# A two-layer streaming encoder on one core: the first MLP's down projection in seven products, one residual tile, and conditioning sums moved and widened

## The chip, the cores and the metric

The kernel runs on one core of one Trainium2 chip. The metric is the device time of one execution in microseconds (us), as the median of several executions of the same program. The core has five engines that run side by side, each with its own instruction stream in a fixed order: PE (matrix products, with PEld for its weight loads), DVE (elementwise work on 128 partitions), ACT (functions and copies), POOL, and SP, which here issues the transfers (DMA) between the chip's memory and the core's on-chip memory. An engine takes its instructions strictly in order: one that waits holds everything behind it. Instructions wait on semaphores that other engines raise.

## What is computed

The reference is one inference step with two layers over 1024 prompt rows and 32 sample rows of width 1024, all in float32. What matters here:

```python
def ada_mod(c, w, b):
    return jax.nn.silu(c) @ w + b
...
    for l in range(DEPTH):
        sh1, sc1, g1, sh2, sc2, g2 = jnp.split(ada_mod(c, p['w_ada'][l], p['b_ada'][l])[:, None, :], 6, axis=-1)
        u = x * (1 + sc1) + sh1
        ...
        x = layer_norm(ALPHA * x + (1 + g1) * y, p['ln_g'][l, 0], p['ln_b'][l, 0])
        u = x * (1 + sc2) + sh2
        f = jnp.square(jax.nn.relu(u @ p['w_up'][l])) @ p['w_down'][l]
        x = layer_norm(ALPHA * x + (1 + g2) * f, p['ln_g'][l, 1], p['ln_b'][l, 1])
```

Layer 0 mixes with a chunked matrix memory, layer 1 with banded attention that reads keys and values made from `ada_mod(c, w_ada_kv, b_ada_kv)`. Both layers end in the same MLP: up from 1024 to 4096 columns, squared relu, down to 1024. There are two conditioning vectors c, one for the prompt rows and one for the sample rows, so every `ada_mod` is a product of a 1024 x n matrix with two vectors; layer 1's matrix has 6144 columns and the keys' one 2048.

## The kernel before

All activations are kept transposed: 128 partitions hold a slice of the features, and the 1056 rows lie along the free axis. Float32 accuracy on PE is bought with three matmuls for each product: operands are split into a high and a low part, and high x high, high x low and low x high are accumulated (`proj`, line 111). PE works on 128 x 128 weights and a moving tile of up to 384 rows.

The order in time is: mixer of layer 0; its output projection (`out_proj` at line 1371); MLP of layer 0; queries, keys and values; attention; output projection of layer 1; MLP of layer 1; output norm.

MLP of layer 0 (`mlp`, line 1006) is plain. It takes the 4096 hidden columns in eight groups of 512. For each group it computes `up` on row blocks of 384, 384 and 288 (`TBS`), squares, splits into high and low, and multiplies by the group's part of w_down (`down`), which DVE adds into the residual: `add_gated_at`, line 986, one instruction for each result in PSUM. The hidden values stay on chip.

MLP of layer 1 (`mlp7`, line 1124) works on quarters of 264 rows (`QN`). Its up writes the hidden values of 14 of the 16 column blocks, already combined into the seven forms that a seven-product (Strassen-like) 2 x 2 scheme needs, to the chip's memory (`hd`), and the last two blocks plainly (`up_plain`, to `hpl`). Its down then runs in 16 units: four groups of column blocks (3, 4, 3 and 4 of them: `GRP`) times four pairs of output columns. `forms` (line 1217) loads a unit's weights (`rdn`) and makes their seven combinations with DVE and ACT; `fill` loads the hidden forms (`fx`) into room on chip that has come free, some of it the room of the up's input; `unit` (line 1263) issues seven products for each of two row pairs, and after each of them DVE adds its PSUM result into the residual. A product into a PSUM bank that DVE is still to read must wait for it. The two plain blocks follow at the end. PE's order within the 16 units is as written (`manual_schedule`), DVE, ACT and SP get theirs when the program is built.

The conditioning of layer 1 and of the keys is made during the MLP of layer 0, on DVE, because PE is busy (`ada_cols`, line 225, called by `ada_rest`, line 1373): 1 MB of weights comes for two column chunks of 128, in two loads; for each of eight blocks of 128 weight rows and both vectors one instruction of 256 columns multiplies and accumulates; then one transpose and one reduce. After every fourth pair four tiny matmuls on PE (`adas`, line 252) sum over partitions. The values go into `ada`, the norm's gains and shifts (`combine`) follow, and `bias_table` makes the attention's bias.

Such work is cut into pieces by a small planner, `Flow` (line 47). A task is a generator that yields a number; the main program calls `flow.tick(us)` after each of its own products. A tick subtracts its amount from the waits, and a task whose wait has come to zero or below goes one step and gets its next wait whole: what it was over is not carried on.

```python
            t[1] -= us
            if t[1] <= 0:
                wait = next(t[0], self)
                ...
                    t[1] = wait or 0.0
```

`flow.finish(task)` runs all that is left of a task at once, at that place of the program. The norms are such tasks too (`norm`, line 846), and `before0(ti)` and `end0` finish them where their result is needed.

The residual of layer 0 (`open_acc`, line 800) is three tiles, one for each row block, each in a pool of its own that closes when that block's norm is done. Their room is used again by the query tiles `QO`. Temporaries come from a pool of five tiles (`tmp_t`), raw weights from three (`raw_tile`), split weights from six.

## Time and profile before

| | us |
|---|---|
| median of 3 runs | 2479.84 |
| lowest and highest of them | 2478.87, 2482.77 |
| the profiled execution, its own time | 2483.94 |
| its span in the profile | 2482.1 |

The stages of the profiled execution, by the busy time of the engines in each:

| stage | from, to (us) | PE busy | DVE busy | ACT busy | DMA share |
|---|---|---|---|---|---|
| mixer of layer 0 | 0 to 421 | 401.07 | 354.29 | 221.88 | 0.41 |
| its output projection | 421 to 517.5 | 95.61 | 78.76 | 40.59 | 0.38 |
| queries | 1266 to 1362 | 95.31 | 77.35 | 62.95 | 0.30 |
| keys and values | 1362 to 1426 | 60.56 | 44.19 | 35.52 | 0.34 |
| attention | 1426 to 1640 | 201.49 | 147.65 | 136.09 | 0.12 |
| output projection of layer 1 | 1640 to 1733 | 88.99 | 53.48 | 43.24 | 0.32 |
| end of the last down, output norm | 2412 to 2482 | 56.56 | 52.15 | 15.09 | 0.29 |

The rows of the two MLPs, which stand between these, are shown where they are used. To read the views: a group of instructions is given by its line in the kernel, engine, operation, the tile it writes and the tiles it reads, the shape, how many there were (x), their busy time together, the mean length of one in ns, and the idle time of the engine ahead of them with what ended it. A matmul's length is from its start to its modelled end, and the next one starts before that: what a run of matmuls costs is its length in time divided by their count. A stage's row gives for each engine the busy time and the number of instructions, then the granted clock of PE, the share of the DMA engines' time and the bytes moved. In the chain of waits and in the timeline the first two numbers are start and length in us.

### The profile page before, as it was taken

The numbers are of one execution on the slowest core, as the hardware profiler recorded it, in microseconds if no ns is written. First come the engines' busy times: TensorE is split into PE (matmuls) and PEld (weight loads), VectorE is DVE, ScalarE is ACT, GpSimd is POOL, SyncE is SP. The second block draws the span as 40 slices with busy tenths as digits, with TensorE's granted clock in tenths as the row PEclk, the third lists the DMA queues.
The fourth block names the chain that finished last, engine by engine and source line by source line (L and its number), as shares of the span: only waits on it lengthen the run. The fifth ranks groups of instructions, "written<-read, shape, count | busy, mean of one in ns | idle before, by whom it ended". The sixth has DMA issues, their size and how long they took to land.

```text
span 2482.1 us, 42688 instructions
## 1 busy us (share of the span) xinstructions
PE 2416.0 (97%) x16844; PEld 2317.8 (93%) x16844; DVE 1764.3 (71%) x4046; ACT 1011.6 (41%) x2110; POOL 166.3 (7%) x315
## 2 busy tenths in 40 slices
PE   7999999999999999999999999999999999899997
PEld 4999999999999999999999967789999999899997
DVE  4899899788679679677597667746853443776758
ACT  4544456382212212212266566654754443221212
POOL 0211100000000000000000144410000000000003
PEclk9999999999999999999999999999999999999999
DMA  8433233313224224234122310051376557667632
GB/s 294 124 109 96 82 93 112 126 35 113 80 88 135 85 87 132 81 94 142 43 96 83 90 41 1 18 147 34 133 248 218 204 180 276 233 243 270 257 129 72
DMA packets 236220, 318.10 MB, mean 128 GB/s; under 512 B 11624, under 2 KB 185084, under 8 KB 234996
## 3 DMA queue, kind: packets, MB, share of 16 engines
q1 hardware_dynamic: 236020, 315.38, 38.8%
q8 instruction: 132, 2.16, 0.4%
q14 instruction: 68, 0.56, 0.1%
HBM read 242.79 MB, written 74.91 MB: 128 GB/s over the span
## 4 chain that ended last, share of the span: by engine, by line
PE 78%; DVE 8%; DMA 6%; ACT 2%; issue 1%; POOL 0%; SPq 0%; DVEq 0%; ACTq 0%; POOLq 0%
PE up L118 9%; PE up L120 9%; PE up L119 9%; PE dn L1278 9%; PE dn L119 5%; PE dn L118 5%; PE dn L120 5%; DMA fx<-hd 3%; PE pv L1599 2%; PE pt L1579 2%; PE s L1549 2%; PE o L118 1%; PE o L119 1%; PE o L120 1%; PE op_b L118 1%
## 5 line engine op out<-in xcount | busy, mean ns | idle before, releaser
L120 PE MATMUL up<-u,w_up 128*128 128x264 f32 x1024 | 292.9, 286 | 0.0
L118 PE MATMUL up<-u,w_up 128*128 128x264 f32 x1024 | 292.4, 286 | 0.0
L119 PE MATMUL up<-u,w_up 128*128 128x264 f32 x1024 | 291.1, 284 | 0.0
L1278 PE MATMUL dn<-fx,wf 128*128 128x264 f32 x2208 | 274.7, 286 | 10.7 <-DVE s L1242 8.0
L1278 PEld LDWEIGHTS dn<-fx,wf 128*128 128x128 f32 x2208 | 272.3, 190 | 11.9 <-DVE s L1242 8.1
L119 PE MATMUL dn<-h,w_dn 128*128 128x384 f32 (+1 forms) x768 | 249.5, 325 | 0.0
L118 PE MATMUL up<-U,w_up 128*128 128x384 f32 (+1 forms) x768 | 249.2, 324 | 0.0
L119 PE MATMUL up<-U,w_up 128*128 128x384 f32 (+1 forms) x768 | 247.9, 323 | 0.0
L118 PE MATMUL dn<-h,w_dn 128*128 128x384 f32 (+1 forms) x768 | 247.8, 323 | 0.0
L120 PE MATMUL up<-U,w_up 128*128 128x384 f32 (+1 forms) x768 | 247.6, 322 | 0.0
L120 PE MATMUL dn<-h,w_dn 128*128 128x384 f32 (+1 forms) x768 | 247.3, 322 | 0.0
L119 PEld LDWEIGHTS up<-u,w_up 128*128 128x128 f32 x1024 | 193.9, 189 | 0.0
L118 PEld LDWEIGHTS up<-u,w_up 128*128 128x128 f32 x1024 | 193.8, 189 | 0.0
L120 PEld LDWEIGHTS up<-u,w_up 128*128 128x128 f32 x1024 | 193.3, 189 | 0.0
L238 DVE SCALAR_TENSOR_TENSOR aacc<-rada,cs,aacc 128x256 f32<-128x256 f32 x448 | 190.2, 477 | 0.0
L986 DVE SCALAR_TENSOR_TENSOR ACC<-dn,ada,ACC 128x264 f32<-128x264 f32 (+4 forms) x328 | 131.8, 426 | 81.5 <-PE dn L1278 69.0
L986 DVE SCALAR_TENSOR_TENSOR acc<-dn,ada,acc 128x384 f32<-128x384 f32 (+2 forms) x256 | 119.4, 486 | 47.0 <-PE dn L120 45.9
L119 PEld LDWEIGHTS dn<-h,w_dn 128*128 128x128 f32 x768 | 144.5, 188 | 0.2 <-DVE h L1028 0.2
L1025 ACT ACTIVATE r<-up 128x384 f32<-128x384 f32 (+1 forms) x96 | 44.2, 462 | 246.3 <-PE up L120 237.7
L120 PEld LDWEIGHTS dn<-h,w_dn 128*128 128x128 f32 x768 | 144.5, 188 | 0.0
L120 PEld LDWEIGHTS up<-U,w_up 128*128 128x128 f32 x768 | 144.3, 188 | 0.0
L118 PEld LDWEIGHTS up<-U,w_up 128*128 128x128 f32 x768 | 144.2, 188 | 0.1
(354 smaller groups left out, 5959.7 us busy)
## 6 DMA issues: line engine op xcount, KB each, us to landing
hd<-HL SPq DMA_DIRECT2D x28, 1848.0 KB
raw_up<-in_w_up_dram SPq DMA_DIRECT2D x68, 512.0 KB
rada<-in_w_ada_dram SPq DMA_DIRECT2D x64, 512.0 KB
fx<-hd SPq DMA_DIRECT2D x37, 528.0 KB
raw_dn<-in_w_down_dram SPq DMA_DIRECT2D x36, 512.0 KB
ada_room<-in_w_ada_dram SPq DMA_DIRECT2D x32, 512.0 KB
fx<-hd SPq DMA_DIRECT2D x50, 264.0 KB
fx<-hd SPq DMA_DIRECT2D x16, 792.0 KB
```

The source lines that it names most:

```text
L118: nc.tensor.matmul(ps, wh, mov(0, k), start=(k == 0), stop=False)
L119: nc.tensor.matmul(ps, wh, mov(1, k), start=False, stop=False)
L120: nc.tensor.matmul(ps, wl, mov(0, k), start=False, stop=(k == nk - 1))
L238: nc.vector.scalar_tensor_tensor(acc[:, cnd], raw[:, k], sc, acc[:, cnd], op0=ALU.mult, op1=ALU.add)
L986: nc.vector.scalar_tensor_tensor(xs, ps[:, off + o:off + o + mm_], gate[:, fc, cnd:cnd + 1], xs, op0=ALU.mult, op1=ALU.add)
L1025: nc.scalar.activation(r, ps[:, :n], AF.Relu)
L1278: nc.tensor.matmul(p, ws[w][:, wl, k], t[:, s0, xl], start=first and k + n_ == 0, stop=k == kg - 1 and n_ == 2, skip_group_check=not first)
L1549: nc.tensor.matmul(s[:, b, :w], qst, kk[i][:, g, k0 + j0:k0 + j0 + w], start=(i == 0), stop=(i == 1))
L1579: nc.tensor.transpose(pt[:kp, j - j0, pr * P:(pr + 1) * P], ps_[pr][:, j * P:j * P + kp], ident)
L1599: nc.tensor.matmul(pv[64 * e:64 * e + 64, :nq], V[:kp, vt0 + j, g * 64:(g + 1) * 64], pts[e][:kp, j, :nq], start=(j == 0), stop=(j == nt - 1))
```

## The change

The first MLP uses `mlp7` as well, through a class `L0` that tells it where its input, rooms and row pairs are; `mlp` and `open_acc` go. The residual of layer 0 is one tile `ACC0` of 1056 rows, and its pool closes when all three norms are done, ahead of the second row block of the queries. Conditioning is made by a new function in three parts: 24 chunks of layer 1 and the keys' 16 during the first up (four chunks at once, 512 columns in an instruction, one load of 256 KB for each of the eight blocks of 128 weight rows), 16 chunks during the first down (two at once, 256 columns, a load of 256 KB for two of these blocks), and 8 during the second up (four at once). The order in `mlp7` between up and down and the time at which a unit's weights are asked for (`step`) change for both layers, and `forms` writes two of its sums over the raw weights.

```diff
+    def ada_more(src, c0, base, nch, nb, mk, tmp_f, step):
+        n = nb * P
+        kk_ = 512 // n
+        for j in range(0, nch, nb):
...
+            for k0 in range(0, KC, kk_):
+                raw = tmp_f([P, kk_, n], f"rada_{base}_{j}_{k0}")
+                nc.sync.dma_start(raw, src[k0 * P:(k0 + kk_) * P, c0 + j * P:c0 + (j + nb) * P].rearrange(
+                    "(k p) c -> p k c", p=P))
+                yield step[0]
+                for k in range(kk_):
+                    for cnd in range(2):
+                        sc = cs[:, k0 + k, cnd:cnd + 1]
+                        if k0 + k:
+                            nc.vector.scalar_tensor_tensor(accs_[cnd], raw[:, k], sc, accs_[cnd],
+                                                           op0=ALU.mult, op1=ALU.add)
...
+            yield step[1]
+            ada_sums(at, base, j, nb, mk)
...
-    ADA_B = (4.0, 2.0, 1.0)
+    ADA_U, ADA_D, ADA_1 = (3.2, 2.0), (7.5, 1.5), (6.0, 2.0)
-    W00 = (6.0, 12.0, 0.0, 0.0, 0.0, 3.0)
+    W00 = ((6.0, 12.0, 0.0, 0.0, 0.0, 3.0), (6.0, 12.0, 0.0, 0.0, 0.0, 3.0), (16.0, 14.0, 0.0, 0.0, 0.0, 3.0))
...
-            nc.vector.tensor_sub(s3, a11, a21)
-            nc.vector.tensor_sub(s4, a12, s2)
-            for x, y in ((s2, s1), (s3, s4)):
+            nc.vector.tensor_sub(a11, a11, a21)
+            nc.vector.tensor_sub(a12, a12, s2)
+            for x, y in ((s2, s1), (a11, a12)):
...
-        for pb in range(NW, NPB):
-            up_plain(pb, tp0)
+        for tp in L.pairs:
+            up_plain(NW, tp)
         prep(0)
+        up_plain(NW + 1, tp0)
+        for _ in range(4):
+            got[0] = next(preps[0])
+        prep(1)
         for t in L.rooms(tp0):
             rooms.add(t)
         fill(0, fx)
-        up_plain(NW, tp1)
-        for _ in range(4):
-            got[0] = next(preps[0])
         up_plain(NW + 1, tp1)
-        prep(1)
         for t in L.rooms(tp1):
             rooms.add(t)
         fill(0, fx)
+        L.down()
         with tc.manual_schedule(engines={mybir.EngineType.PE}):
...
-                    if j == 3:
+                    if j == 4:
                         prep(i + 2)
...
+    def ada_up():
+        yield from ada_more(a["w_ada"][1], 0, 48, 24, 4, mm, tmp_t, ADA_U)
+        yield from ada_more(a["w_ada_kv"], 0, 96, 16, 4, mm, tmp_t, ADA_U)
...
+        bias_table()
+    def ada_down():
+        yield from ada_more(a["w_ada"][1], 3 * D, 72, 16, 2, mm, tmp_t, ADA_D)
...
+    def ada_last():
+        yield from ada_more(a["w_ada"][1], 5 * D, 88, 8, 4, mm, tmp_t, ADA_1)
...
     def before0(ti):
         flow.finish(norms[ti])
         if ti == 2:
-            norms["ada"] = flow.add(ada_rest())
+            norms["ada"] = flow.add(ada_up())
...
+    class L0:
+        l, alloc, add, gate, wups = 0, mm, add_gated_at, ada_part(0, 5), wup0
+        pairs, quarters, blocks = (0, 1), (0, 1, 2, 3), TBS
+        ready, after = before0, end0
...
+        def down():
+            flow.finish(norms["ada"])
+            norms["ada"] = flow.add(ada_down())
...
+    mlp7(L0)
...
                 flow.finish(norms[ti])
-                acc_cm[ti].__exit__(None, None, None)
+                if ti == 1:
+                    flow.finish(norms[2])
+                    acc_cm0.__exit__(None, None, None)
...
+            if i == 2:
+                norms["ada"] = flow.add(ada_last())
+        def down():
+            flow.finish(norms["ada"])
```

`ada_sums` issues the four `adas` matmuls once eight chunks are complete and adds their result into `ada`. In `mlp7` a tile of the up ends with `flow.tick(264 / 96)`, and a product of the down with `flow.tick(264 * kg / 768)`, kg being the 3 or 4 column blocks of its group. `L.ready(0)` stands ahead of the first quarter's six tiles of the up, `L.ready(1)` ahead of the second quarter's six, and `L.ready(2)` eight tiles later; there are 128 tiles in all.

## What was predicted before the change was run

> **What bounds the kernel now.** First the page, then a table by stage.
>
> ```profile
> span 2482.1 us, 42688 instructions
> ...
> PE 2416.0 (97%) x16844; PEld 2317.8 (93%) x16844; DVE 1764.3 (71%) x4046; ACT 1011.6 (41%) x2110; POOL 166.3 (7%) x315
> ...
> PE 78%; DVE 8%; DMA 6%; ACT 2%; issue 1%; POOL 0%; SPq 0%; DVEq 0%; ACTq 0%; POOLq 0%
> ```
>
> PE bounds it: 97% busy, 78% of the chain that ended last. Fewer matmuls pay in full where PE stays fed, and a wait put into PE's stream costs in full. The stages that change (first MLP, second up, start of the second down, rest of it):
>
> ```profile
> 517.50:1266.00 748.50, 748.44 (x4683) 746.08 (x4683) 556.37 (x1194) 203.87 (x354) 0.00 (x0) 1.00 0.30 93
> 1733.00:2111.00 378.00, 377.75 (x3076) 377.53 (x3077) 188.94 (x263) 188.20 (x302) 0.00 (x0) 1.00 0.60 211
> 2111.00:2142.00 31.00, 21.49 (x151) 20.87 (x150) 19.50 (x43) 8.29 (x19) 0.00 (x0) 0.83 0.81 292
> 2142.00:2412.00 270.00, 268.76 (x2206) 268.18 (x2205) 191.61 (x423) 55.85 (x99) 0.00 (x0) 1.00 0.59 213
> ```
>
> The first MLP leaves PE no gap, so no stall can be saved there, only matmuls. The start of the second down is different: 31 us with PE idle for nine of them.
>
> **Part 1, fewer matmuls: -36 us.** Pitch is length by count: 748.50 / 4683 = 0.1598 us for the mixed 384 and 288 rows; 378.00 / 3076 = 0.1229 for 264 rows in an up; 270.00 / 2206 = 0.1224 in a down. The first MLP has 2304 up and 2304 down matmuls. After: 3072 x 0.1229 = 378 (up), 4 x 14 column blocks x 7 products x 2 row pairs x 3 = 2352 x 0.1224 = 288 (seven products), 8 x 4 x 3 x 3 = 288 x 0.1598 = 46 (plain rest). Together 712 against 748.5.
>
> **Part 2, the conditioning's first part does not fit into the up.** This decides the sign. A tile of the up ticks 264/96 = 2.75. The wait of 3.2 between loads isn't met by one tick, and nothing is carried over, so each of a group's eight loads takes two tiles, and the 2.0 behind them one: 17 tiles. Ten groups need 170. The task starts at `ready(2)`, 20 of the 128 tiles being done; 108 remain: six groups (102 tiles) and the first loads of the seventh. `down()` then finishes the rest at once. The order in which the changed program's instructions stand agrees: on DVE, between the third and the fourth PSUM result of the first unit, stand 62 multiply-adds of 512 columns (31 loads, two vectors), eight transposes and eight reduces; on PE two sets of `adas` matmuls stand behind the third product, waiting for those reduces, and every later matmul queues behind them. So PE stands still until DVE is through. The prices on DVE:
>
> ```profile
> 431.42 3.25 DVE L238 SCALAR_TENSOR_TENSOR ada_room<-ada_room,cs 128x256 f32<-128x256 f32 x8
> 436.66 0.62 DVE L978 SCALAR_TENSOR_TENSOR acc<-op_a,ada,acc 128x384 f32<-128x384 f32 x1 [0.24 <-DMA acc<-xsp]
> 2122.05 0.49 DVE L986 SCALAR_TENSOR_TENSOR ACC<-dn,ada,ACC 128x264 f32<-128x264 f32 x1 [0.61 <-PE dn L1278]
> ...
> L245 DVE STREAM_TRANSPOSE aat<-aacc 128x512 f32<-128x512 f32 x32 | 22.6, 706 | 0.3
> L246 DVE TENSOR_REDUCE cx<-aat 128x16 f32<-128x512 f32 x32 | 21.7, 679 | 0.2
> ```
>
> 256 columns back to back cost 3.25 / 8 = 0.41 us. No 512-column one is in the trace; this kind of instruction grows by (0.62 - 0.49) / 120 = 1.08 ns a column, so 0.41 + 0.28 = 0.68. Bounds: 0.41 (columns free) and 0.81 (twice). I take 0.68: the slope is measured on the same operation. The first two loads are asked for early and count with the front below; the other 29 give 58 x 0.68 + 8 x (0.70 + 0.66) = 39 + 11 = 50 us of DVE.
>
> The loads come on top. Of five temporaries two hold sums, so three loads are in flight; a new one is issued when DVE has read the one three back, and after a group's last multiply-adds the next group's first load starts afresh.
>
> ```profile
> 930.94 4.00 DMA raw_up<-in_w_up_dram
> 1364.86 5.52 DMA x<-xsp
> ...
> raw_up<-in_w_up_dram SPq DMA_DIRECT2D x68, 512.0 KB
> ```
>
> 512 KB took 4.00 us in a quiet stretch and 5.52 in a busy one; a load of 256 KB lies between half the first (2.0) and the second. I take 3.3, nearer the row for twice the bytes than to half of it. Then three loads, 2 x 0.68 = 1.36 us of DVE each, go round in 3.3 + 1.36 = 4.66 us against 4.08 of DVE, and a group boundary exposes about 1 us: 2 to 3 us a group, about 9 in all. At 2.0 it is 0, at 5.5 about 30. Ahead of it, PE stops 3.3 us after the up's end (three products of 9 x 0.1224), while DVE has splits of the last up tiles and of weights in line, SP holds the next loads behind the transfer of such a split, and the first then lands: about 10 us (6 to 13). Stall: 10 + 50 + 9 = 69 us, bounds 56 to 93.
>
> The Trainium skill, "DMA: Bandwidth & Descriptors", section on the anatomy of one DMA, gives a fixed part of about 2.0 us plus bytes by 436 GB/s. That is 2.6 us for 256 KB, and 3.2 for 512 KB where the row has 4.00; by it the stall would be an estimated 61 us.
>
> **Part 3, after the stall.** How PE starts again shows at the second down:
>
> ```profile
> 2111.29 2.35 PE L1278 MATMUL dn<-fx,wf 128*128 128x264 f32 x18
> 2115.19 11.22 PE L1278 MATMUL dn<-fx,wf 128*128 128x264 f32 x90 [1.55 <-ACT hl L89]
> 2134.37 7.79 PE L1278 MATMUL dn<-fx,wf 128*128 128x264 f32 x39 [7.96 <-DVE s L1242]
> ```
>
> After 7.96 us of idleness 39 matmuls took 7.79 us instead of 4.8: +3 us, bounds 1 and 3. The skill, "TensorE: Matmul & The Clock Gate", Part 1, has half rate after an idle window of 3.4 us and full rate after a busy one of that length, an estimated 1.7 us; the granted clock of that stretch, 0.83, agrees with the mechanism, and the row is the larger. The second unit's weights, held behind the flush on DVE, and the fourth result cost 3 more (0 to 5).
>
> **Part 4, DVE in the first down.** The second down's DVE was busy 191.61 of 270.00 us, 71%. The first one gets seven to eight groups of `ada_down` besides, each 16 x 0.41 + 0.70 + 0.66 = 7.9 us: 60 us in 288, so 92%. What it can take:
>
> ```profile
> DVE ACC L986 <- PE dn L1278: 61.5, 88, 2.0
> DVE s L1240 <- DMA rdn<-in_w_down_dram: 7.3, 6, 1.9
> ```
>
> DVE had 61.5 us of idling for PE, just the 60 that are added. Blocks of four (1.6 us) delay results for which PE has three half products of time (12 x 0.1224 = 1.5 us each), but DVE will also wait for loads that SP holds behind `fx` transfers, and weights are asked for one product later. From 0 to 25; I take 9. In the second down the later asking alone: 0 (0 to 8), for DVE idles there.
>
> **Part 5, the second down starts better: -11 us.** 18 + 90 + 39 matmuls are 18.0 us at 0.1224, and took from 2111.29 to 2142.16: 13 lost. The stop was for `s`, made of the second unit's weights:
>
> ```profile
> 2110.09 15.80 SPq L1189 DMA_DIRECT2D hpl<-hl  x4
> 2125.99 1.59 SPq L1223 DMA_DIRECT2D rdn<-in_w_down_dram  x2
> ```
>
> Their load stood in SP's queue behind transfers that waited for the last up tiles. In the new order it stands ahead of these, and ahead of most of the `fx` loads, whose last ones then come later. 3 to 13; I take 11.
>
> **Part 6, small moves.** In the up of layer 0 DVE gets about 6.5 groups, each 16 x 0.68 + 2.7 = 13.6 us, 88 on top of the 188.94 of 378 that the second up shows: 73%, hidden by three tiles of hidden values that PE can run ahead; with that cover gone, each late load would hold the up back. The second up gets two groups, 27 us: 57%. Nothing for both. At the seam to the queries the first norm had 264 matmuls ahead of its reader (42 us at 0.1598), now it has 192 (31 us) and needs 27 of the 28 ticks in them; and the queries' second block now waits for the whole residual's room: 0 to 12, by eight PSUM banks of 24 matmuls of cover I take 3. One residual tile: its first load waits for the same engines as before, so 0.
>
> **Sum** against the profiled span: 2482.1 - 36 + 69 + 3 + 3 + 9 - 11 + 3 = 2522. The median of the runs is 2.3 us under that span (2479.84), so 2520.
>
> **Rivals.** (a) *The flush is short, and the kernel faster.* Its decisive point is a stall of 36 + 13 + 0 - 3 = 46 us with every small cost at its bound. That needs 0.41 us for 512 columns and quiet loads (58 x 0.41 + 11 = 35) and no more than 3 us at the front: stall 38, span 2482.1 - 36 - 13 + 38 + 3 = 2474. So 2472. For it: the first loads can land while PE still runs. Against it: the slope of 1.08 ns. 6%. (b) *DVE bounds the first down*: the 92% turn into waits, each late load holding PSUM results; 25 to 60 us in place of 9, so 2536 to 2571. For it: DVE's order is fixed and mixes the two streams; against: the 61.5 us. 12%. (c) *Narrow matmuls eat the gain*: the mean lengths are nearly as large for 264 rows as for 384.
>
> ```profile
> L118 PE MATMUL up<-u,w_up 128*128 128x264 f32 x1024 | 292.4, 286 | 0.0
> L118 PE MATMUL up<-U,w_up 128*128 128x384 f32 (+1 forms) x768 | 249.2, 324 | 0.0
> ```
>
> If cost went with them, the up's 3072 would cost 3072 x 286 / 324 = 2712 old ones (+65 us), the down's 2352 + 288 come to 2364 (+10), in place of -36: 2520 + 36 + 75 = 2631. The pitches refute it: 1%. (d) *Gains and stall cancel*, at a stall of about 45 us with small costs: 2475 to 2485; 4%.
>
> **How the numbers follow.** The forecast, a stall of 55 to 90 us that outweighs both gains, has 77%. Low end: stall 56, other costs at their least, 2482 - 36 + 56 + 1 - 13 = 2490; high end: stall 85 with 15 for DVE and 8 at the seam, 2557. The range 2490 to 2556 leaves out (a), (c), (d) and most of (b). About 0.2% (5 us) is what a measurement here tells from no change: faster 6%, same 4%, slower 90%.
>
> **What would show it.** One PE gap of 55 to 90 us some 4 us into the first down, ended by `adas`; DVE rows of 512 columns near 680 to 750 ns; a first up and down whose matmuls have pitches of 0.122 to 0.123; no 8 us stop in the second down. It is wrong if that gap is under 45 us or lies elsewhere, or if DVE's waits for `rada` in the first down cost PE more than 25 us.

## The result, and the profile after

The changed kernel takes 2574.1 us (median of 4 runs, 2572.84 to 2575.94) against 2481.3 for the kernel before: a ratio of 1.037, interval 1.0357 to 1.0382. The direction was predicted; the size was not: 2520 with a range up to 2556. The profiled execution's span is 2571.8, against a sum of 2522 in the prediction, so 50 us are to be accounted for.

The page of the changed kernel, the lines that answer to those of before:

```profile
span 2571.8 us, 45523 instructions
...
PE 2392.4 (93%) x17948; PEld 2291.0 (89%) x17948; DVE 1841.0 (72%) x4034; ACT 1088.9 (42%) x2226; POOL 164.8 (6%) x315
...
PE 72%; DVE 11%; DMA 9%; ACT 2%; issue 1%; SPq 0%; POOL 0%; DVEq 0%; ACTq 0%; POOLq 0%
```

PE was busy 97% and is now busy 93%; in the chain of waits DVE and DMA took over what PE lost. Where, the busy times by stage show: first up, the flush, the rest of the seven products, then the second down's start and its remainder, and last three pieces of the flush. A transfer's time is counted where it starts, so the DMA share of a short stretch can pass 1.

```profile
517.30:892.90 375.60, 374.96 (x3102) 374.36 (x3101) 244.13 (x366) 192.71 (x320) 0.00 (x0) 1.00 0.69 238
892.90:982.80 89.90, 5.26 (x46) 4.63 (x44) 60.96 (x99) 5.65 (x14) 0.00 (x0) 0.53 0.65 218
982.80:1300.20 317.40, 293.62 (x2338) 290.74 (x2335) 261.48 (x607) 61.70 (x109) 0.00 (x0) 0.97 0.61 214
...
2197.90:2229.00 31.10, 22.46 (x153) 21.32 (x153) 20.43 (x46) 8.65 (x18) 0.00 (x0) 0.84 0.98 347
2229.00:2501.80 272.80, 268.66 (x2202) 267.93 (x2202) 191.75 (x422) 55.89 (x99) 0.00 (x0) 1.00 0.57 210
...
893.00:911.00 18.00, 4.58 (x28) 4.09 (x26) 9.27 (x18) 4.92 (x12) 0.00 (x0) 0.64 1.04 367
911.00:925.00 14.00, 0.00 (x0) 0.00 (x0) 6.27 (x10) 0.63 (x1) 0.00 (x0) 0.50 0.78 266
925.00:983.00 58.00, 0.78 (x17) 0.64 (x18) 45.42 (x73) 0.00 (x0) 0.00 (x0) 0.50 0.49 161
```

The up took 375.6 us (378 predicted) with PE fed throughout. In the flush PE did 27 matmuls of the seven products, 3.3 us of work, in 89.9: 86.6 lost. The other 2325 of 2352 matmuls, 284.6 us of work at 0.1224, took 317.4: 32.8 lost. The second down, from its first product to its plain rest, took 303.9, where the one before took 300.9.

PE's largest waits over the whole execution (total, times, longest, in us):

```profile
PE adas L266 <- DVE cx L304: 81.7, 3, 49.2
PE adas L266 <- DVE cx L309: 11.5, 1, 11.5
PE dn L1238 <- DVE ACC L1025: 11.5, 9, 3.5
```

The first row is the wide groups' reduces: 81.1 us of it are the flush, 0.6 the end of the up. The second is new to the argument: the narrow groups of the first down (`ada_down`) bring `adas` matmuls too, and one set of these held PE for 11.5 us. Of the third, 8.4 us lie in the first down behind the flush and 3.1 in the second down. Two stretches of the timeline, PE in the flush, and DVE at the flush's first loads and around that second wait:

```profile
898.84 2.32 PE L1238 MATMUL dn<-fx,wf 128*128 128x264 f32 x9 [3.58 <-issue]
950.39 0.31 PE L266 MATMUL adas<-cx,sel 128*32 128x16 f32 x8 [49.23 <-DVE cx L304]
982.53 0.31 PE L266 MATMUL adas<-cx,sel 128*32 128x16 f32 x8 [31.83 <-DVE cx L304]
982.77 6.10 PE L1238 MATMUL dn<-fx,wf 128*128 128x264 f32 x33
988.71 8.25 PE L1238 MATMUL dn<-U,wf 128*128 128x264 f32 x66
```

```profile
911.49 1.41 DVE L295 SCALAR_TENSOR_TENSOR aacc<-rada,cs,aacc 128x512 f32<-128x512 f32 x2 [6.36 <-DMA rada<-in_w_ada_kv_dram]
...
922.11 4.22 DVE L295 SCALAR_TENSOR_TENSOR aacc<-rada,cs,aacc 128x512 f32<-128x512 f32 x6 [6.41 <-DMA rada<-in_w_ada_kv_dram]
...
1149.93 0.56 DVE L90 TENSOR_TENSOR wf<-rdn,wf 128x384 fp32r<-128x384 f32 x1 [4.24 <-ACT wf L89]
...
1153.49 1.67 DVE L295 SCALAR_TENSOR_TENSOR aacc<-rada,cs,aacc 128x256 f32<-128x256 f32 x4
...
1155.94 0.69 DVE L309 TENSOR_REDUCE cx<-aat 128x16 f32<-128x512 f32 x1
```

PE stood 3.58 + 49.23 + 31.83 = 84.6 us around the third product, where the prediction had put the stop. Up to 1149.93 DVE, in its fixed order, waited 4.24 us for ACT's split of late weights, and behind that stood the group's last multiply-adds and the reduce for which PE's `adas` waited.

Why the flush was longer than its DVE work: DVE's groups and waits in it, then one load's issue by SP, and pieces of the chain of waits through the flush (start, length; for a transfer from its issue to its landing).

```profile
L295 DVE SCALAR_TENSOR_TENSOR aacc<-rada,cs,aacc 128x512 f32<-128x512 f32 x56 | 38.6, 748 | 20.9 <-DMA rada<-in_w_ada_kv_dram 20.6
L303 DVE STREAM_TRANSPOSE aat<-aacc 128x512 f32<-128x512 f32 x8 | 5.2, 687 | 0.0
L304 DVE TENSOR_REDUCE cx<-aat 128x16 f32<-128x512 f32 x8 | 5.0, 660 | 0.0
L298 DVE TENSOR_SCALAR aacc<-rada,cs 128x512 f32<-128x512 f32 x8 | 3.5, 484 | 3.7 <-DMA rada<-in_w_ada_kv_dram 3.7
```

```profile
901.37 0.62 SPq L288 DMA_DIRECT2D rada<-in_w_ada_kv_dram  x1
...
902.52 10.40 DMA hpl<-hl
...
916.65 5.36 DMA rada<-in_w_ada_kv_dram
...
931.82 5.66 DMA rada<-in_w_ada_kv_dram
...
954.72 2.97 DMA rada<-in_w_ada_kv_dram
```

The work itself is 38.6 + 5.2 + 5.0 + 3.5 = 52.3 us, against 50 predicted. The loads cost 20.6 + 3.7 = 24.3, against 9, and 13.6 of this fell into the first of the four groups (waits of 6.36, 6.41, 0.28 and 0.56). Two things made that group late. A load issued at 901.37, beside the loads of hidden forms and at a DMA share of 1.04, was still waited for at 911.4, some 10 us later. And the next three stood in SP's queue until 916.65, behind a store of the plain blocks that waited for the one before it to land, 10.40 us. Loads that were issued at 916.65 and 931.82 still took 5.36 and 5.66 us; those on the chain after 939, with the last load of hidden forms issued at 930.42, took 2.94 to 3.48, and the other three groups waited 10.7 us together.

### The profile page after: what moved, and what is told of

Read it like the earlier page. It is cut to its first block, busy times and chain, and to the rows that moved or that the text cites. A ratio compares the mean times of both kernels' runs of the same rounds, so it can differ in the third digit from the quotient of the medians.

```text
span 2571.8 us, 45523 instructions
## 1 busy us (share of the span) xinstructions
PE 2392.4 (93%) x17948; PEld 2291.0 (89%) x17948; DVE 1841.0 (72%) x4034; ACT 1088.9 (42%) x2226; POOL 164.8 (6%) x315
## 3 DMA queue, kind: packets, MB, share of 16 engines
q1 hardware_dynamic: 277476, 432.11, 49.4%
## 4 chain that ended last, share of the span: by engine, by line
PE 72%; DVE 11%; DMA 9%; ACT 2%; issue 1%; SPq 0%; POOL 0%; DVEq 0%; ACTq 0%; POOLq 0%
PE dn L1238 17%; PE up L120 9%; PE up L118 9%; PE up L119 9%; PE pv L1609 2%; DMA fx<-hd 2%; PE pt L1589 2%; PE s L1559 2%; DMA rada<-in_w_ada_kv_dram 2%; PE o L118 1%; PE o L120 1%; PE o L119 1%; DVE aacc L295 1%; DVE wf L90 1%; DMA U<-hd 1%
## 5 line engine op out<-in xcount | busy, mean ns | idle before, releaser
L1238 PE MATMUL dn<-fx,wf 128*128 128x264 f32 x3108 | 407.6, 288 | 23.0 <-DVE ACC L1025 7.3
L1238 PEld LDWEIGHTS dn<-fx,wf 128*128 128x128 f32 x3108 | 393.7, 191 | 26.2 <-issue 16.4
L1025 DVE SCALAR_TENSOR_TENSOR ACC<-dn,ada,ACC 128x264 f32<-128x264 f32 (+5 forms) x648 | 263.9, 432 | 154.8 <-PE dn L1238 129.1
L118 PE MATMUL up<-U,w_up 128*128 128x264 f32 x1024 | 291.5, 285 | 0.0
L119 PE MATMUL up<-U,w_up 128*128 128x264 f32 x1024 | 291.0, 284 | 0.0
L120 PE MATMUL up<-U,w_up 128*128 128x264 f32 x1024 | 290.0, 283 | 0.0
L120 PEld LDWEIGHTS up<-U,w_up 128*128 128x128 f32 x1024 | 192.8, 188 | 0.0
L119 PEld LDWEIGHTS up<-U,w_up 128*128 128x128 f32 x1024 | 192.4, 188 | 0.0
L118 PEld LDWEIGHTS up<-U,w_up 128*128 128x128 f32 x1024 | 192.2, 188 | 0.1
L295 DVE SCALAR_TENSOR_TENSOR aacc<-rada,cs,aacc 128x512 f32<-128x512 f32 (+1 forms) x280 | 167.1, 642 | 35.1 <-DMA rada<-in_w_ada_kv_dram 20.6
L1238 PE MATMUL dn<-U,wf 128*128 128x264 f32 x1308 | 179.4, 287 | 4.9 <-DVE ACC L1025 3.5
L1238 PEld LDWEIGHTS dn<-U,wf 128*128 128x128 f32 x1308 | 168.7, 190 | 6.3 <-ACT wf L89 2.1
L90 DVE TENSOR_TENSOR HL<-H,HL 128x264 fp32r<-128x264 f32 x112 | 125.2, 1118 | 29.7 <-ACT HL L89 29.2
L90 DVE TENSOR_TENSOR w_up<-raw_up,w_up 128x1024 fp32r<-128x1024 f32 x72 | 87.9, 1223 | 77.3 <-ACT w_up L89 77.3
```

Of the source, the lines that this page charges most:

```text
L90: (eng or nc.vector).tensor_sub(dst_l, src, dst_h.bitcast(F32))
L118: nc.tensor.matmul(ps, wh, mov(0, k), start=(k == 0), stop=False)
L119: nc.tensor.matmul(ps, wh, mov(1, k), start=False, stop=False)
L120: nc.tensor.matmul(ps, wl, mov(0, k), start=False, stop=(k == nk - 1))
L295: nc.vector.scalar_tensor_tensor(accs_[cnd], raw[:, k], sc, accs_[cnd], op0=ALU.mult, op1=ALU.add)
L1025: nc.vector.scalar_tensor_tensor(xs, ps[:, off + o:off + o + mm_], gate[:, fc, cnd:cnd + 1], xs, op0=ALU.mult, op1=ALU.add)
```

## The experiments

All times are medians beside the kernel before on the same chip; stage lengths are taken from the first matmul of a stage to that of the next in the profiled execution ("first down" without its plain rest, which is 47.5 to 49.2 everywhere).

| run | us | ratio to before, interval | first up | first down | queries to second up | second down |
|---|---|---|---|---|---|---|
| changed kernel | 2574.1 | 1.0357 to 1.0382 | 375.6 | 407.3 | 472.1 | 303.9 |
| e1_fit | 2513.5 | 1.0116 to 1.0148 | 393.8 | 331.0 | 471.6 | 308.2 |
| e2_fit_late | 2505.7 | 1.0078 to 1.0108 | 393.6 | 321.7 | 468.6 | 305.5 |
| e3_fit_nodown | 2494.4 | 1.0027 to 1.0061 | 393.3 | 309.7 | 474.2 | 305.1 |
| e4_more_flush | 2597.3 | one run | 374.5 | 436.5 | 468.6 | 304.7 |
| e5_before_neworder | 2482.1 | 0.9991 to 1.0008 | | | | 302.4 |
| e6_fit_oldorder | 2507.2 | 1.0079 to 1.0109 | 393.6 | 327.0 | 473.1 | 303.0 |
| e7_flush_first | 2555.9 | one run | 380.0 | 387.4 | 470.6 | 304.7 |
| e8_late_both | 2502.3 | 1.0066 to 1.0094 | 388.0 | 327.5 | 468.4 | 304.1 |
| e9_nocond | 2471.5 | 0.9945 to 0.9974 | 375.4 | 307.2 | 470.9 | 304.1 |
| e10_spread | 2496.0 | 1.0039 to 1.0072 | 384.2 | 310.6 | 485.4 | 304.5 |
| e11_noloads | 2545.7 | 1.0246 to 1.0277 | 374.8 | 384.3 | 469.7 | 305.2 |
| e12_pool | 2565.4 | 1.0327 to 1.0368 | 441.5 | 334.3 | 468.7 | 301.7 |
| e13_defer | 2561.2 | 1.0296 to 1.0353 | 371.7 | 399.2 | 468.4 | 304.3 |

Profiled executions lie up to 8 us from their medians: those of e1_fit, e3_fit_nodown, e6_fit_oldorder and e10_spread are the slowest of their four, those of e2_fit_late, e8_late_both, e9_nocond and e13_defer the fastest of theirs. In e7_flush_first and e13_defer the last 24 matmuls of the up, some 3 us, come behind the first products of the down and count with it.

**The flush taken away.**

```diff
-    ADA_U, ADA_D, ADA_1 = (3.2, 2.0), (7.5, 1.5), (6.0, 2.0)
+    ADA_U, ADA_D, ADA_1 = (2.7, 2.0), (7.5, 1.5), (6.0, 2.0)
```

> One number is changed: the wait between two loads of the conditioning in the first up, 3.2, becomes 2.7, so that each tile of the up (2.75) takes one load; a group then needs 9 tiles, ten groups 90 of the 108. The same work is done, and nothing is left for the flush. Theory (the flush in PE's order is what cost most): the stop of 49.2 + 31.8 us at `adas` and the slow restart behind it (3) go, the rest of the first down still loses its 30: 2574 - 84 = 2490, between 2482 and 2500. Rival (the DVE work costs wherever it stands): DVE's 244 us of 376 in the up become about 244 + 50, and late loads of conditioning hold the hidden tiles' splits: the up grows by 25 to 60 us, 2515 to 2550.

2513.5, between the two: the first down lost 76 us of its length, but the up gained 18. The waits of PE up to the first product, and ACT at that place:

```profile
PE dn L1238 <- ACT wf L89: 6.7, 1, 6.7
PE adas L266 <- DVE cx L304: 6.7, 3, 3.8
```

```profile
910.52 0.63 ACT L89 CAST hl<-hr 128x528 fp32r<-128x528 f32 x1 [16.41 <-DMA hpl<-hl]
911.48 0.51 ACT L89 CAST wf<-rdn 128x384 fp32r<-128x384 f32 x1 [0.33 <-DMA rdn<-in_w_down_dram]
```

In the up, which now had ten wide groups in place of six, `adas` too waited for reduces, 6.7 us, with slow matmuls behind them. And the start of the down, which in the changed kernel disappears within the flush, came into sight: ACT stood idle for 16.4 us until a store, which landed among the loads of hidden forms, freed its buffer, and the first weights were split only after that. So the flush is the largest cause, but moving it into the up won 61 us, not the 85 of the stop.

**`adas` later in the first down.** On top of e1_fit:

```diff
-    ADA_U, ADA_D, ADA_1 = (2.7, 2.0), (7.5, 1.5), (6.0, 2.0)
+    ADA_U, ADA_D, ADA_1 = (2.7, 2.0), (6.0, 9.0), (6.0, 2.0)
```

> As e1_fit, and in the first down the four `adas` matmuls are issued 9 ticks behind their reduce instead of 1.5 (the waits between loads go from 7.5 to 6.0, so that the task still ends in the down). Theory (in the first down too, PE's order holds a matmul that waits for a reduce on DVE, and the 11.5 us wait is the `adas` one): that wait goes, 11 us below e1_fit, some 2479. Rival (the late weights behind which DVE stood for 4.2 us are what holds PE, and the stop only moves to the first product that needs them): within 4 us of e1_fit.

The first down shortened by 9.3 us and the median fell by 7.8. The `adas` wait of the first down, 11.8 us in e1_fit, is gone, as the theory said; part of the time saved came back as waits for the residual adds, 11.1 us in place of 6.6 in e1_fit:

```profile
PE dn L1238 <- DVE ACC L1025: 11.1, 9, 2.5
```

**No conditioning in the first down.**

```diff
-        yield from ada_more(a["w_ada"][1], 3 * D, 72, 16, 2, mm, tmp_t, ADA_D)
+        nc.vector.memset(ada[:, 72:88, :], 0.0)
+        yield 1.0
```

> As e1_fit, with the 16 column chunks of conditioning in the first down left out (their 128 multiply-adds, 32 loads, transposes, reduces and two sets of `adas`; these values are set to zero). It prices what they cost the first down. Theory (the 30 us that the first down loses behind the flush come from that work: DVE at 80 to 93%, the `adas` wait): 25 to 30 us below e1_fit, about 2462. Rival (the weights come late because their loads stand in SP's queue behind the loads of hidden forms, conditioning or not): no more than 10 us below e1_fit.

The first down became 21.3 us shorter than in e1_fit (the medians differ by 19.1), so `ada_down` costs some 20 there: nearer the theory's 25 to 30 than the rival's 10. It still took 309.7 for 288 of matmuls; most of that rest is its start:

```profile
PE dn L1238 <- DMA U<-hd: 6.4, 2, 5.8
PE dn L1238 <- ACT wf L89: 6.3, 1, 6.3
```

**A longer flush.**

```diff
-    ADA_U, ADA_D, ADA_1 = (3.2, 2.0), (7.5, 1.5), (6.0, 2.0)
+    ADA_U, ADA_D, ADA_1 = (5.6, 2.0), (7.5, 1.5), (6.0, 2.0)
```

> As the changed kernel, with the wait between loads in the up at 5.6, which takes three tiles a load: 32 more multiply-adds of 512 columns, two more groups, are left to the flush. It splits the stop into a front and a price for each group. By the last three groups of the changed kernel (15.8 to 17 us each, 13.9 of it DVE's) the stop grows by 2 x 16.4 = 33 us: 2607, between 2600 and 2614. Rival (the stop is mostly a front, contention with the loads of hidden forms, and a group more costs no more than DVE's time while these loads still run): 25 or less, below 2599.

The first down grew by 29.2 us, 14.6 for a group; 2597.3 lies just on the rival's side. It is one run, but its trace agrees with the price of a group: the last four start 16.0 us apart (946.3, 962.4, 978.3, 994.4), which is the prediction's 13.6 of DVE and 2 to 3 of loads. The first group's loads were waited for 5.9 us here in place of 13.6, which more than covers that the down grew by 29 and not by 32. So what the prediction lacked lies at the front, and not in the price of a group.

**The flush ahead of the last loads of hidden forms.**

```diff
+        L.down()
         prep(1)
...
-        L.down()
         with tc.manual_schedule(engines={mybir.EngineType.PE}):
```

> As the changed kernel, with the flush issued ahead of the second unit's weights and of the loads into the room of the up's input. It asks why the flush took some 15 us longer than predicted: DVE waited 24 us for its loads in place of 9. Theory (the first loads, 10 us each, shared the DMA engines with those of hidden forms, share 1.04): DVE's waits for `rada` in the flush are below 14 us, though the time need not fall, for the hidden forms then come behind the flush, up to 20 us of new waits for them. Rival (256 KB takes that long at three loads in flight): the waits stay at 20 to 26 us.

The theory's number failed: DVE still waited 21.7 us for loads of the flush (9.78 of it once, at a DMA share of 0.90 in that stretch), while loads into `U` were landing beside its groups. The first group, now ahead of them, waited 3.1 us in place of 13.6, and the second had the 9.78: the wait went with the hidden forms' loads, and was not of the flush's own making.

```profile
923.93 0.88 DVE L298 TENSOR_SCALAR aacc<-rada,cs 128x512 f32<-128x512 f32 x2 [9.78 <-DMA rada<-in_w_ada_kv_dram]
```

The time fell by 18 all the same, in one run: 79.0 us were waited at `adas` of the wide groups in place of 81.7, and the 11.5 us wait of the first down is gone, with no change to `ada_down`. That suggests that this wait depends on where a reduce happens to fall beside late weights.

**The flush without its loads.**

```diff
-                raw = tmp_f([P, kk_, n], f"rada_{base}_{j}_{k0}")
-                nc.sync.dma_start(raw, src[k0 * P:...
+                if nb == 2 or k0 == 0:
+                    raw = tmp_f([P, kk_, n], f"rada_{base}_{j}_{k0}")
+                    nc.sync.dma_start(raw, src[k0 * P:...
```

> The changed kernel with seven of the eight loads of each wide group left out (the same 256 KB tile is multiplied eight times, so DVE does all of its work and these values are wrong). It prices the loads in the stop: DVE idled 24 us for them there, 13.6 of it in the first of the four groups. Theory (the loads are what the prediction undersized: 24 where it had 9 and part of the front's 10): the two `adas` waits, 81 us together, fall to 60 to 68, the time by 13 to 20, to 2554 to 2561. Rival (what is late at the front is DVE's and SP's other work at the seam, and the loads only fill the gaps): the waits stay above 72, the time above 2566.

PE's waits in the flush, and DVE's timeline:

```profile
PE adas L266 <- DVE cx L306: 46.1, 2, 26.0
PE dn L1240 <- issue: 14.7, 1, 14.7
```

```profile
916.80 0.88 DVE L299 TENSOR_SCALAR aacc<-rada,cs 128x512 f32<-128x512 f32 x2 [6.38 <-DMA rada<-in_w_ada_kv_dram]
917.60 9.36 DVE L296 SCALAR_TENSOR_TENSOR aacc<-rada,cs,aacc 128x512 f32<-128x512 f32 x14
...
930.75 9.36 DVE L296 SCALAR_TENSOR_TENSOR aacc<-rada,cs,aacc 128x512 f32<-128x512 f32 x14
```

The stop is 46.1 + 14.7 = 60.8 in place of 84.6: 23.8 us went with the loads. (The expectation's figure was for `adas` alone; part of the stop now shows as "issue", so the sums are compared.) DVE's waits for loads in the flush fell from 24.3 to 7.0, of which 6.38 stand at the front for the one load that a group keeps: 17.3 us of the 23.8. Where the other 6.5 come from isn't shown. The time fell by 28.4, more than the 13 to 20 expected. A group is now 930.75 - 917.60 = 13.15 us of DVE and nothing else.

**`adas` later, the same flush.** The keys' sixteen chunks reduce into tiles of their own, and their sums are issued some fifteen half products into the down.

```diff
-        yield from ada_more(a["w_ada_kv"], 0, 96, 16, 4, mm, tmp_t, ADA_U)
+        yield from ada_more(a["w_ada_kv"], 0, 96, 16, 4, mm, tmp_t, ADA_U, True)
...
     def ada_down():
+        yield 14.0
+        for i in range(2):
+            ada_sums(None, 96, 8 * i + 4, 4, mm, cxk[i])
```

> The changed kernel with the same flush on DVE, but with the two sets of `adas` that stood behind the third product issued some fifteen half products later, from a small tile of their own. It asks what holds PE in the stop: the place of `adas` in PE's order, or DVE's queue, in which the residual adds stand behind the flush so that PSUM results aren't read. Theory (DVE's queue: PE may run on until its PSUM banks are full or until the next `adas`, a dozen half products of 1.1 us): 10 to 16 us faster than the changed kernel, 2558 to 2564. Rival (the place of `adas` alone): the stop of 85 us all but goes, below 2510.

2561.2, within the theory's band: 13 us faster. PE's timeline:

```profile
912.09 1.00 PE L1240 MATMUL dn<-U,wf 128*128 128x264 f32 x3 [6.96 <-DMA U<-hd]
...
957.38 0.31 PE L267 MATMUL adas<-cxk,sel 128*32 128x16 f32 x8 [27.02 <-DVE cxk L305]
```

PE ran on for some hundred matmuls, waited for hidden forms (14.1 us in seven waits over the whole first down, five of them on this way), and stood at the moved `adas` for 27.0 and 31.6, for these still came before the flush was done. A later place saves what PE can do until then; whether DVE's residual adds would have stopped it without any `adas` isn't shown, for it never got so far.

**The order between up and down.** In the kernel before, only the new order in `mlp7` (as the change's diff has it) and the later asking for weights:

```diff
-                    if j == 3:
+                    if j == 4:
```

> The kernel before, with only the new order between up and down and the later asking for weights (product 4 in place of 3) in the second MLP. Prediction's Part 5: the 8 us stop for the second unit's weights goes, -11: 2471, between 2468 and 2478. Rival, from the changed kernel's trace (its second down starts with 22.66 us of PE in 31.3, and waits for `fx` in place of weights; the same 14 loads of hidden forms must land at a DMA share of 0.98): the stop only changes its name, and the room that the up's input frees comes later: +3, between 2482 and 2489.

No difference: 2482.1 against 2482.6. The start of its second down:

```profile
2114.55 9.26 PE L1278 MATMUL dn<-fx,wf 128*128 128x264 f32 x72 [1.37 <-issue]
...
2127.06 1.33 PE L1278 MATMUL dn<-fx,wf 128*128 128x264 f32 x9 [1.54 <-DMA fx<-hd]
2131.84 18.32 PE L1278 MATMUL dn<-fx,wf 128*128 128x264 f32 x133 [3.45 <-DMA fx<-hd]
```

The 7.96 us stop for weights is gone, as predicted. In its place stand waits for `fx`, 7.4 us over the whole down, where the kernel before had 0.9:

```profile
PE dn L1278 <- DMA fx<-hd: 7.4, 4, 3.5
```

The same edit the other way round, both parts put back in both MLPs of e1_fit:

> As e1_fit, with the order between up and down, and the asking for weights at product 3, put back as in the kernel before, for both MLPs. Theory (the start of both downs is held by the loads of hidden forms, and the new order frees the first row pair's room later): about 4 us in each down, so 8 below e1_fit: 2505, between 2499 and 2510. Rival (prediction's Part 5: the new order saves the stop for weights): 11 us in each above e1_fit, some 2530. Third (the loads set the start whatever the order): within 4 us of 2513.

6 us faster than e1_fit, at intervals of some 4 us each way, with a first down 4.0 us shorter and a second 5.2: the theory's direction and size, though with the null result of e5 the order alone can't be given a price in the second MLP.

**The first MLP without any conditioning.**

```diff
-        yield from ada_more(a["w_ada"][1], 0, 48, 24, 4, mm, tmp_t, ADA_U)
-        yield from ada_more(a["w_ada_kv"], 0, 96, 16, 4, mm, tmp_t, ADA_U)
+        nc.vector.memset(ada[:, 48:72, :], 0.0)
+        nc.vector.memset(ada[:, 96:112, :], 0.0)
+        yield 2.0
```

and the edit of e3_fit_nodown.

> The changed kernel with all of the conditioning of the first MLP left out: the 24 and 16 chunks of its up and the 16 of its down (their values are set to zero). It measures the first MLP in seven products by itself, prediction's Part 1 (712 us in place of 748.5 where nothing stalls), and what the start of its down costs. Theory (a start like the second MLP's, 13 us lost to the loads of hidden forms, and nothing else): up 376, down 301, rest 48, so 725; from there on as in the changed kernel (+5 and +3): 2482 - 23 + 8 = 2466, between 2460 and 2473. Rival (the 22 us that the run without `ada_down` still lost in its first down belong to the seven products there, not to conditioning): 735 and 2476 or more.

```profile
515.60:891.00 375.40, 373.98 (x3079) 373.77 (x3078) 178.35 (x246) 194.32 (x328) 0.00 (x0) 1.00 0.58 206
891.00:1198.20 307.20, 294.54 (x2355) 291.99 (x2353) 210.88 (x460) 63.60 (x113) 0.00 (x0) 0.98 0.64 229
```

375.4 + 307.2 + 47.5 = 730.1 us against 748.5 before, and 2471.5 lies within the theory's range. With no conditioning at all the seven products gain 18 us there, and 3.7 and 3.2 are given back at the queries and in the second down; the whole kernel is 10 us faster than before, by 0.26 to 0.55%. About that is the most that a better placing of the conditioning could win in this form of the kernel.

**Three attempts to place it better.** On top of e2_fit_late:

```diff
-    ADA_U, ADA_D, ADA_1 = (2.7, 2.0), (6.0, 9.0), (6.0, 2.0)
+    ADA_U, ADA_D, ADA_1 = (2.7, 5.4), (6.0, 9.0), (6.0, 2.0)
```

> As e2_fit_late, and in the first up too the `adas` matmuls are issued two tiles behind their reduce (5.4 in place of 2.0; a group takes 10 tiles, ten groups 100 of the 108). In e1_fit the up was 18 us longer than in the changed kernel: 6.7 of waits at `adas`, some 3 to 4 of slower matmuls behind them, and 6.7 at the first unit's weights. Theory (a matmul in PE's order that waits for a reduce costs its wait and a slow restart): the first two go, 8 to 10 us below e2_fit_late: 2497, between 2493 and 2500. Rival (DVE was late in the up because it is full, so that the wait moves to the next result that DVE must read): within 3 us of 2506.

The up is 5.6 us shorter and the first down 5.8 longer: its start waited once for 10.7 us for a load into `U`. The theory's waits did not go: PE waited 9.4 us at the up's `adas`, 6.6 in e2_fit_late, for the last reduce now came 7.0 us late. What went from the up is the 6.5 us wait for the first unit's weights, which were ready by then.

```profile
PE dn L1238 <- DMA U<-hd: 17.2, 5, 10.7
```

The median is 3.4 lower, near the rival's 3. The time moved to the next thing that was late at the seam. With the early start, the old order and a tail in the queries:

```diff
-        if ti == 2:
+        if ti == 1:
             norms["ada"] = flow.add(ada_up())
...
     def ada_down():
+        yield 30.0
...
     def end0(blk):
-        flow.finish(norms["ada"])
```

and `ADA_U`, `ADA_D` at (2.7, 5.4) and (7.5, 9.0).

> All the work is done, spread as the runs so far suggest: the up's conditioning starts with the second quarter and takes one load a tile, its `adas` stand two tiles behind their reduce and end 14 tiles earlier, ahead of the loads of hidden forms; the down's starts 30 ticks late, takes longer waits and may run on through the queries; order and asking as in the kernel before. Theory (what is left to lose is contention at the seam and `adas` in PE's order): up 377, down 305, rest 48: 730, then +5 and 0: 2469, between 2464 and 2485. Rival (DVE's work as a whole bounds it, some 200 us of conditioning on 437 of the rest in 715, and in the queries too): no better than 2490.

The rival: 2496.0. The first down came to 310.6, close to what was hoped, but the up to 384.2, and the stretch from the queries to the second up took 13 us more, for DVE's work went on there. That DVE's work as a whole is the bound isn't shown: it was busy for 299 of 384 us in the up and 249 of 311 in the down, and PE's largest waits in that down were for loads into `U`, 13.1 us, 10.2 of them at once. Half of the multiply-adds on POOL:

```diff
+                            if cnd:
+                                nc.gpsimd.tensor_scalar(raw[:, k], raw[:, k], sc, 1.0, op0=ALU.mult, op1=ALU.mult)
+                                nc.gpsimd.tensor_add(accs_[cnd], accs_[cnd], raw[:, k])
+                            else:
```

and `ADA_U`, `ADA_D` at (2.7, 2.7) and (6.0, 6.0), with one wait more ahead of a group's reduces.

> All the work is done, with order, asking and the early start of the up's conditioning as in e10_spread, the down's conditioning kept inside the down, and the multiply-adds of the second conditioning vector moved from DVE to POOL, which idles there (a product of 512 columns took it 0.69 us, an add 1.45: 2.1 for what costs DVE 0.71). DVE gets some 95 us less in the first MLP. Theory (conditioning costs there by DVE's time and by matmuls that wait for its reduces): first MLP 376 + 308 + 48 = 732, q and later as in the changed kernel: 2475, between 2468 and 2483. Rival (POOL's work slows DVE or comes later than a tile's 2.95 us, and the loads at the seam remain): no better than e10_spread, 2490 or more.

2565.4, the rival, and worse than any other placing without a flush. DVE's and POOL's groups, and PE's wait:

```profile
L299 DVE SCALAR_TENSOR_TENSOR aacc<-rada,cs,aacc 128x512 f32<-128x512 f32 x70 | 68.6, 980 | 34.9 <-DMA rada<-in_w_ada_kv_dram 17.6 <-DMA rada<-in_w_ada_dram 16.9
```

```profile
L297 POOL TENSOR_TENSOR aacc<-aacc,rada 128x512 f32<-128x512 f32 x70 | 105.7, 1510 | 5.8
L296 POOL TENSOR_SCALAR rada<-rada,cs 128x512 f32<-128x512 f32 x70 | 89.8, 1282 | 118.6 <-DVE aacc L299 118.6
```

```profile
PE adas L266 <- DVE cx L311: 45.6, 5, 15.6
```

Instructions of both engines took longer than alone (last section), and the groups came so late that the last row, PE's wait at `adas`, grew to 45.6 us in five; the up took 441.5. None of these three versions beats the kernel before.

## Why the prediction was right in direction and wrong in size

The sign came from Part 2, and that mechanism came true. The time lies above the range because three terms of the sum were too small or had the wrong sign: the loads of the flush in Part 2, what follows the flush in Part 4, and the second down in Part 5.

**Part 1** holds for the matmuls: the up took 375.6 (378), the plain rest 47.9 (46), and the pitch was 375.6 / 3072 = 0.1223, with 0.1229 used. But the 288 for the seven products was pure matmul time. The second down's rows had shown that such a down loses 13 us at its start, to weights and hidden forms; e9_nocond lost 19 in its first one. In the changed kernel the flush covers the start, so this didn't enter the error, but even without any conditioning the whole gain was 10 us (e9_nocond), where rival (a) set 46 against the stall.

**Part 2** holds in mechanism and place: one stop behind the third product, ended by `adas`, multiply-adds of 38.6 / 56 = 0.69 us each (0.68 taken). Its failed term is the loads: "about 9 in all" at 3.3 us each, which were 24.3, 13.6 of them in the first of the four groups. The stop was 86.6 with its slow matmuls, in place of 69: 17.6 of the 50 us, 15.3 of them loads and 2.3 DVE's work; the 10 for the front was right. e11_noloads shows the size: 17.3 us less of DVE's waits, and 23.8 us less stop. For the other three groups 3.3 was near: after their first loads, those on the chain took 2.94 to 3.48 us. The error was to use it for the first group too, for the flush begins just when the hidden forms' loads fill the engines, at a DMA share of 1.04; the row that the prediction called busy, 5.52 us for 512 KB, had a share of 0.54 around it. Its bounds, up to 30 us for the loads, held the number, and DVE's 24.3 us lie just under the 25 that it named as a sign of being wrong. That SP holds loads behind a plain block's store was seen, and priced too low.

**Part 3** had 3 us for the restart. 33 matmuls started at 982.77, and the next at 988.71: 5.94 us in place of 4.0, so 1.9; behind the 11.5 us wait it was the same, 24 matmuls in 4.81 us in place of 2.94. The Trainium skill, "TensorE: Matmul & The Clock Gate", Part 1, has half rate until a busy window of 3.4 us has passed, an estimated 1.7; the granted clock of 0.50 in the stop agrees, and this was nearer than the 3 us that the prediction took from a row.

**Part 4** is the second failed term. Parts 3 and 4 had 15 us for what follows the flush; it was 32.8. The prediction priced DVE's load and late results, but not that `ada_down`'s own `adas` matmuls stand in PE's order and wait for a reduce: the mechanism of Part 2 again, in small. That wait was 11.5, with 1.9 of slow restart; in e1_fit, where it was 11.8, it disappears by a later issue (e2_fit_late, 9.3 us less) or by leaving the work out (e3_fit_nodown, 21.3 less). Waits for residual adds took 8.4 more, waits for hidden forms and weights 3.8, the restart behind the flush 1.9; the remaining 5 of the 32.8 aren't explained. Rival (b) had 25 to 60 us in place of Part 4's 9: with 32.8 - 1.9 = 31 its size came true beside the stop, by way of `adas` more than of residual adds.

**Part 5** is the third: -11 predicted, +3 measured in the changed kernel. The stop for weights did go. But the loads of hidden forms must land in the same stretch, at a DMA share of 0.98, and whichever was asked for later became the stop: e5_before_neworder shows that exchange alone, worth nothing. The prediction had written that the last `fx` loads would come later, and had charged nothing for it. In e5 the second down is 1.5 us longer than before; the other half of the 3 isn't explained.

**Part 6** holds: the stretch from the queries to the second up grew by 4.9 (3 taken, up to 12), and both ups cost nothing for their groups. In e1_fit four more groups lengthened the up by 18, but not as "with that cover gone" had it: PE waited at `adas` (6.7) and for the first unit's weights (6.7), and not for hidden tiles.

In sum: 17.6 for the stop (15.3 of it loads), 17.8 behind it (`adas` of the narrow groups, residual adds), 14 in the second down (hidden forms in place of weights, 1.5 of it unexplained): 49.4 of 49.8; the other stages differ from the sum by little.

## What to carry to other kernels

A matmul that sums another engine's late result holds everything behind it in PE's order, so it belongs as far behind that result as the engine's work allows. Issuing it later won 9.3 us of a wait of 11.8 where the result was ready by then (e2_fit_late), and none of the waits at `adas` where the result came later still (e8_late_both). A stop for one transfer in a stretch where the DMA engines are full was worth nothing by reordering here, for the next transfer in line took its place (e5_before_neworder); and work that is flushed into such a stretch is priced by rows from a stretch as full, not from quieter ones. The work of the other engines has to be placed before the matmuls saved on the bottleneck engine are counted: here the best that its placing could win was about 10 us.

## What was not expected of the hardware

DVE and POOL slow each other. A multiply by a scalar on POOL, from the changed kernel's attention:

```profile
L1575 POOL TENSOR_SCALAR p<-p,mx 128x512 f32<-128x512 f32 x8 | 5.6, 694 | 4.3 <-DVE mx L1574 4.2
```

In e12_pool a DVE multiply-add of 512 columns took 980 ns, 748 by the same kind of row in the changed kernel's flush, where POOL does nothing; the POOL multiply took 1282 ns in place of these 694. Inside the first MLP of e12_pool the overlap in time shows it too: 27 of the 70 multiply-adds had next to no POOL work beside them and took 747 ns on average, the 29 that were covered by POOL's work 1062; 21 of POOL's 70 multiplies had DVE idle beside them and took 695, the 35 that were covered 1730. The Trainium skill, "SBUF — State Buffer", section "Who interferes with whom", says that a DVE instruction with two inputs on chip contends with a POOL instruction that reads there; these rows agree in kind.

A store of 528 KB took 10.40 us to land, and loads of 256 KB between 2.94 and some 10, within one stretch of 80 us. The Trainium skill, "DMA: Bandwidth & Descriptors", anatomy of one DMA, gives a fixed part of about 2.0 us plus bytes by 436 GB/s, for transfers that POOL issues; by it an undisturbed load of 256 KB would be an estimated 2.6. These are issued by SP, and the fastest of them comes near it.
